# A two-layer hybrid backbone on one core: modulation with its weight stationary, and matmul operands at another place in SBUF

## The chip, the cores and the metric

The kernel runs on one core of a Trainium2 chip. A core has five engines that run side by side: TensorE (PE, with the weight loads shown apart as PEld), VectorE (DVE), ScalarE (ACT), GpSimd (POOL) and SyncE (SP), which here only issues DMA transfers between main memory (HBM) and the on-chip memory SBUF; matmuls write to PSUM. A matmul has a stationary operand, loaded ahead of it, and a moving one that is streamed through. The metric is device time in microseconds; smaller is better. The kernel before takes 3382.59 us (median of three runs).

## The reference

Two groups of tokens, a prompt of 128 and a latent grid of 1024, share the weights of two layers (D = 1024). Of each layer:

```python
def mix_inputs(x, cond, p):
    mod = jax.nn.silu(cond) @ p["w_mod"] + p["b_mod"]
    shift, scale, gate = jnp.split(mod, 3, axis=-1)
    h = rmsnorm(x, p["g_norm"]) * (1 + scale[:, None, :]) + shift[:, None, :]
    parts = jnp.split(h @ p["w_in"], _in_split_points(), axis=-1)
    return gate, parts
...
    # three mixers fed by the parts: bidirectional RG-LRU, latent attention (MLA), windowed attention (SWA)
    u = (m[:, :, 0] * ((y_rnn * jax.nn.silu(g_rnn)) @ p["w_br_rnn"])
         + m[:, :, 1] * ((y_mla * jax.nn.silu(g_mla)) @ p["w_br_mla"])
         + m[:, :, 2] * ((y_swa * jax.nn.silu(g_swa)) @ p["w_br_swa"]))
    out = u @ p["w_out"]
    x = x + gate[:, None, :] * out
```

The modulation `mod` is a vector of 3072 numbers per group and layer: one row of conditions (two, one for each group) times a weight of 1024 x 3072. A final RMSNorm closes the net. All of it is float32 to the accuracy of float32.

## The kernel before

**Large matmuls.** Each operand is split into a high and a low part in the type fp32r, and a product is three matmuls, hi*hi, hi*lo and lo*hi (`mm3`, L232 to L239). Activations lie with features on the partitions; the 1152 tokens (1024 and 128) are cut into three chunks of 384 columns. So the input projection (`in`) is, for each of its blocks of 128 output features and each chunk, 8 x 3 matmuls with 128 stationary weight columns and 384 moving token columns (`hhi`, `hli`; `hhh`, `hlh` for the last chunk). `wo` is the output projection, `mgrnn`, `mgmla` and `mgs` are the merges of the three branches, `tm` the projections that come out with tokens on the partitions.

**Modulation** (`prepare`, L277). The weight of a layer comes in six blocks c of 512 columns, each in four quarters q of 256 rows (two k of 128): `unit(c, q)`. A unit loads its quarter (512 KB) and runs one `piece`: the condition is the stationary operand, four columns wide, and the weight moves, 512 columns, into one row of PSUM per condition, `ps[0:4, :]`. In fp32 the four columns are two conditions and two columns of zeros (`scf`); in fp32r they are the high and the low parts of the conditions (`sc4`) and the weight comes in high and low parts too. When a block is complete, `finish` copies the four rows out (ACT, L319, tile `mr`), turns them by four transposes on PE (L322, tile `modT`) so that features lie on the partitions, and DVE adds the bias (from L324).

Two kinds of units: layer 0's blocks 0 to 3 (16 units, `direct`, plain fp32, L310) run in the opening, since scale and shift must be there before the first activation `hhi` can be made; a float32 matmul that is no transpose shows as two records on PE. The opening also holds the sums of squares of the norm (`ssi`, L395) and the broadcast of the inverse root (`rbi`, L406), both small float32 matmuls between the units. The other 32 units (layer 0's blocks 4 and 5, the gate, and layer 1's six blocks) are the stream G of `filler()` (L763) in layer 0's RNN stage, fp32r, L313 and L314: every third filler runs one piece, between pieces of the input projection and of the gates of the RG-LRU (`g`).

**Order and memory.** In these stages the order of PE (and of DVE, ACT and POOL in some) is written by hand (`manual_schedule`); SP's, and elsewhere the others', comes from a scheduler that knows which buffers share memory: a load into memory that was another tile's is put behind the last use of that tile. Pools are laid one behind the other, so that each tile's size shifts what follows. In the merge of the RNN branch (L861) the eight parts of y are read; the first four stay in SBUF, the last four are reloaded (`yraw`, L904, from `yr` in HBM), cast (`yh`, ACT) and subtracted (`yl`, DVE). Just before it the last 24 blocks of the input projection are put through a sigmoid (`osg`, L734) and stored (`sg`, L735).

## Time and profile before

| | before |
|---|---|
| time, median of 3 runs | 3382.59 us (3379.35 to 3383.43) |
| span of the profiled execution | 3375.3 us |
| PE busy | 3287.6 us (97%) |
| DVE, ACT, POOL busy | 1820.3, 1551.6, 1450.9 us (54, 46, 43%) |
| matmul records on PE | 19572 |
| mean granted TensorE clock | 0.984 |

The profile shows one execution. It gives no time of its own for it besides the span, which runs from the first to the last instruction; the median is 7.3 us longer. Busy times of PE overlap from one matmul to the next, because matmuls are pipelined, so that a listed duration is longer than the distance from one start to the next. In a row of the timeline stand start and duration in us, engine, line, operation, output <- inputs, size (partitions x stationary columns, partitions x moving columns), count, and in brackets the idle time before it with what ended it. A granted clock of 1.00 is 2.4 GHz, one of 0.50 is 1.2 GHz.

### The profile page before, as it was taken

The page shows a single profiled execution, that of the slowest core. Times are in us where ns is not written, and L with a number is a line of the kernel's source. Part 1 is how long each engine was busy: PE and PEld are TensorE (multiplying, and loading weights), DVE is VectorE, ACT ScalarE, POOL GpSimd, SP SyncE. Part 2 cuts the span into 40 slices and gives each one's busy share as a digit, 9 for nine tenths or more (in the row PEclk, how much of TensorE's full clock was granted, in tenths as well). Part 3 has the DMA queues.
Part 4 walks back from the last instruction along what each step waited for, and adds up shares of the span by engine and source line. Part 5 has one row for each costly group of instructions (what it writes and reads, how often), then busy time and mean ns, then how long its engine had stood idle before and what let it go on. Part 6 is the DMA issues. An engine that isn't in the chain of part 4 may idle for free. (4 is left out here: it accounts for less than half of the span.)

```text
span 3375.3 us, 52189 instructions
## 1 busy us (share of the span) xinstructions
PE 3287.6 (97%) x19572; PEld 3095.7 (92%) x19572; DVE 1820.3 (54%) x3254; ACT 1551.6 (46%) x3061; POOL 1450.9 (43%) x1174
## 2 busy tenths in 40 slices
PE   7999999999999999999999999999999999999998
PEld 4999999999998998778989999999999999977898
DVE  6345443332327888667563444423332588876766
ACT  4344444434226777554243433333341477765532
POOL 3655554433214444445374445333331244434543
PEclk9999999999999999899999999999999999989999
DMA  5333232232441002446432222222244200234563
GB/s 209 100 99 97 95 119 92 94 99 94 153 155 30 25 25 68 125 135 229 169 114 91 77 79 81 81 73 82 85 132 135 86 28 27 51 103 119 171 201 134
DMA packets 246652, 351.06 MB, mean 104 GB/s; under 512 B 73216, under 2 KB 200832, under 8 KB 246144
## 3 DMA queue, kind: packets, MB, share of 16 engines
q1 hardware_dynamic: 246400, 347.74, 32.5%
q8 instruction: 154, 2.52, 0.3%
q14 instruction: 98, 0.80, 0.1%
HBM read 248.88 MB, written 98.78 MB: 103 GB/s over the span
## 5 line engine op out<-in xcount | busy, mean ns | idle before, releaser
L239 PE MATMUL in<-hhi,wh_in 128*128 128x384 f32 x1536 | 524.0, 341 | 6.0 <-ACT osg L734 4.4
L239 PE MATMUL in<-hli,wh_in 128*128 128x384 f32 x1536 | 522.6, 340 | 1.6 <-DVE hli L427 1.6
L239 PE MATMUL in<-hhi,wl_in 128*128 128x384 f32 x1536 | 521.9, 340 | 0.0
L215 POOL TENSOR_TENSOR wl_in<-wr_in,wh_in 128x1024 fp32r<-128x1024 f32 x94 | 235.4, 2506 | 329.3 <-ACT wh_in L209 254.1
L239 PEld LDWEIGHTS in<-hhi,wh_in 128*128 128x128 f32 x1536 | 290.0, 189 | 6.8 <-ACT osg L734 5.0
L239 PEld LDWEIGHTS in<-hli,wh_in 128*128 128x128 f32 x1536 | 289.8, 189 | 3.9 <-DVE hli L427 3.9
L239 PEld LDWEIGHTS in<-hhi,wl_in 128*128 128x128 f32 x1536 | 289.9, 189 | 0.0
L239 PE MATMUL in<-hlh,wh_in 128*128 128x384 f32 x768 | 261.6, 341 | 2.8 <-DVE hlh L427 2.8
L239 PE MATMUL in<-hhh,wl_in 128*128 128x384 f32 x768 | 261.3, 340 | 2.0 <-POOL wl_in L215 2.0
L239 PE MATMUL in<-hhh,wh_in 128*128 128x384 f32 x768 | 261.5, 340 | 0.3 <-ACT osg L734 0.3
L1169 POOL TENSOR_SCALAR p<-p,mx 128x1152 f32<-128x1152 f32 x128 | 158.2, 1236 | 200.9 <-DVE mx L1166 126.4
L1220 DVE TENSOR_TENSOR pl<-pt,ph 128x512 fp32r<-128x512 f32 (+1 forms) x320 | 201.4, 636 | 29.8 <-ACT ph L1216 27.1
L1216 ACT CAST ph<-pt 128x512 fp32r<-128x512 f32 (+1 forms) x320 | 170.1, 552 | 92.4 <-PE pt L1209 87.9
L610 DVE SCALAR_TENSOR_TENSOR r<-r,txl 128x1156 f32<-128x1156 f32 x16 | 31.4, 1962 | 320.9 <-ACT r L609 320.9
L1209 PE MATMUL pt<-ident,p 128*128 128x128 f32 x1152 | 169.7, 274 | 9.5 <-DVE kl L1079 4.1
L734 ACT ACTIVATE osg<-in 128x384 f32<-128x384 f32 x144 | 69.0, 489 | 237.3 <-PE in L239 154.9
L1209 PEld LDWEIGHTS pt<-ident,p 128*128 128x128 f32 x1152 | 133.2, 141 | 32.6 <-DVE pl L1220 10.5
L209 ACT CAST wh_in<-wr_in 128x1024 fp32r<-128x1024 f32 x96 | 99.9, 1044 | 126.2 <-PE in L239 91.6
L1234 PE MATMUL o<-ph,v 128*128 128x256 f32 x576 | 153.2, 293 | 0.0
L239 PEld LDWEIGHTS in<-hlh,wh_in 128*128 128x128 f32 x768 | 145.0, 189 | 4.3 <-DVE hlh L427 4.3
L239 PEld LDWEIGHTS in<-hhh,wl_in 128*128 128x128 f32 x768 | 144.9, 189 | 2.3 <-POOL wl_in L215 2.3
L1234 PE MATMUL o<-pl,v 128*128 128x256 f32 x576 | 145.7, 280 | 0.0
(451 smaller groups left out, 9652.5 us busy)
## 6 DMA issues: line engine op xcount, KB each, us to landing
wr_in<-in_w_fm SPq DMA_DIRECT2D x96, 512.0 KB, 3.6
sg<-osg SPq DMA_DIRECT2D x144, 192.0 KB, 1.9
wr_wm<-in_w_mod SPq DMA_DIRECT2D x32, 512.0 KB, 4.0
wr_wo<-in_w_out SPq DMA_DIRECT2D x32, 512.0 KB, 3.7
yr<-gsil SPq DMA_DIRECT2D x16, 576.0 KB, 2.8
msgrnn<-sg SPq DMA_DIRECT2D x48, 192.0 KB, 2.4
u<-msgrnn SPq DMA_DIRECT2D x48, 192.0 KB, 2.5
qr<-qs SPq DMA_DIRECT2D x36, 256.0 KB, 3.9
```

The costliest lines, as they stand in the source:

```text
L209: nc.scalar.copy(out=hi, in_=src)
L215: eng.tensor_tensor(out=lo, in0=src, in1=f(hi), op=ALU.subtract)
L239: nc.tensor.matmul(ps, x, y, start=n == 0, stop=n == last)
L610: nc.vector.scalar_tensor_tensor(out=rr[d], in0=rr[d], scalar=1.0, in1=tt[d], op0=ALU.add, op1=ALU.mult)
L734: nc.scalar.activation(out=o, in_=ps, func=ACT.Sigmoid)
L1169: nc.gpsimd.tensor_scalar(out=pts[i], in0=pts[i], scalar1=mxs[i][:, 5:6], scalar2=1.0, op0=ALU.mult, op1=ALU.mult)
L1209: nc.tensor.transpose(ps[:, w:w + P], pts[q][:, k * P:(k + 1) * P], ident)
L1216: nc.scalar.copy(out=r["h", j][:, 0:width(j)], in_=r["t", j][:, 0:width(j)])
L1220: nc.vector.tensor_tensor(out=r["l", j][:, 0:width(j)], in0=r["t", j][:, 0:width(j)], in1=f(r["h", j][:, 0:width(j)]), op=ALU.subtract)
L1234: nc.tensor.matmul(O[:, 0:256], V[k][:, h % 4, :], x[:, 256 * i:256 * i + 256], start=k == 0 and e == 0, stop=k == 8 and e == 1)
```

## The change

It has two parts.

**Modulation.** The operands change places: 128 columns of the weight become stationary and the four condition columns move. A `piece` runs over two k, four blocks i of 128 columns and, in fp32r, the two parts of the weight. The result comes out with features on the partitions, `ps[:, 4 * i:4 * i + 4]`, so the copy `mr` and the transposes `modT` go; DVE reads the result as before.

On PE in the opening, layer 0's blocks 0 to 3; `wm` is a quarter of the weight, `scf` the conditions. Before:

```order
L310 MATMUL mod_0_196<-wm_0_119,scf 4x512 x2
L310 MATMUL mod_0_196<-wm_1_121,scf 4x512 x2
L310 MATMUL mod_0_196<-wm_2_125,scf 4x512 x2
L310 MATMUL mod_0_196<-wm_3_127,scf 4x512 x2
L395 MATMUL ssi_228<-ones,ssai_201 128x1 x3
L322 MATMUL modT_0_241<-ident,mr_0_239 128x4 x4
L310 MATMUL mod_1_250<-wm_0_129,scf 4x512 x2
L310 MATMUL mod_1_250<-wm_1_131,scf 4x512 x2
L406 MATMUL rbi_255<-dgi_235,ones 128x128 x3
```

Now:

```order
L314 MATMUL mod_0_200<-scf,wm_0_123 128x4 x8
L314 MATMUL mod_0_200<-scf,wm_1_125 128x4 x8
L314 MATMUL mod_0_200<-scf,wm_2_129 128x4 x8
L314 MATMUL mod_0_200<-scf,wm_3_131 128x4 x8
L392 MATMUL ssi_256<-ones,ssai_217 128x1 x3
L314 MATMUL mod_1_271<-scf,wm_0_133 128x4 x8
L314 MATMUL mod_1_271<-scf,wm_1_135 128x4 x8
L403 MATMUL rbi_288<-dgi_263,ones 128x128 x3
```

Each quarter has eight matmuls of four moving columns in place of two of 512; the small matmuls of the norm stand where they stood, and the transposes are gone.

On PE in the stream, one piece of layer 0's block 4. Before:

```order
L313 MATMUL mod_4_1000<-wh_wm_4_0_930,sc_98 4x512
L314 MATMUL mod_4_1000<-wl_wm_4_0_931,sc_98 4x512
L313 MATMUL mod_4_1000<-wh_wm_4_0_930,sc_98 4x512
L314 MATMUL mod_4_1000<-wl_wm_4_0_931,sc_98 4x512
L239 MATMUL g_0_000_1012<-xh_0_899,wh_lru_0_539 128x384
```

Now the piece is sixteen matmuls, of which the first and last are:

```order
L314 MATMUL mod_4_1072<-sc_102,wh_wm_4_0_1002 128x4
L314 MATMUL mod_4_1072<-sc_102,wl_wm_4_0_1003 128x4
L314 MATMUL mod_4_1072<-sc_102,wh_wm_4_0_1002 128x4
L314 MATMUL mod_4_1072<-sc_102,wl_wm_4_0_1003 128x4
...
L314 MATMUL mod_4_1072<-sc_102,wl_wm_4_0_1003 128x4
```

Four matmuls became sixteen, at the same place among the others; there are 32 such pieces.

**Layout.** A small tile of 96 bytes (`edge`) at the right end, widths of 1216 in place of 1156 and 1160 elements (`AW`), another order of pools (`ep` behind `mdp`, with `rows` and `rope` in it) and a pool of its own for `mx` move the operands of the large matmuls. By the addresses that the two builds give them, before, the moving operands of the input projection and of `wo` begin at 224 bytes mod 256 and their weights at 128, others at 192, 64, 0 or 32, and those of the wide merge at 128; now moving and stationary operands of all large fp32r matmuls are at 128, but for 480 of `mgs`, whose weights stay at 224 (tile starts; the columns read begin at multiples of 256 behind them). No loop over data and no size of a transfer changes by it.

One order changes by it, on SP's queue at layer 0's merge: `sg` are the stores of the gates, `yraw` the reloads of y. Before:

```order
L735 DMA sg_19_470<-osg 128x384
L827 DMA yrb_1_7330<-yr_2_440 128x1152
L827 DMA yrb_1_7330<-yr_3_441 128x1152
L629 DMA yr_7_445<-gsil_7_6672 128x1152
L735 DMA sg_19_470<-osg 128x384 x2
L904 DMA yraw_6_7875<-yr_6_444 128x1152
L904 DMA yraw_7_7879<-yr_7_445 128x1152
L904 DMA yraw_4_7883<-yr_4_442 128x1152
L222 DMA wr_rnn_0_7911<-in_w_br_rnn 128x1024
L735 DMA sg_20_471<-osg 128x384 x3
```

Now:

```order
L732 DMA sg_22_545<-osg 128x384 x3
L732 DMA sg_23_546<-osg 128x384 x2
L845 DMA msgrnn_0_0_8398<-sg_0_523 128x384
L845 DMA msgrnn_0_1_8402<-sg_0_523 128x384
L732 DMA sg_23_546<-osg 128x384
L845 DMA msgrnn_0_2_8406<-sg_0_523 128x384
L901 DMA yraw_6_8275<-yr_6_516 128x1152
L901 DMA yraw_7_8279<-yr_7_517 128x1152
L901 DMA yraw_4_8283<-yr_4_514 128x1152
L907 DMA krt_8295<-in_rope_k 128x512
```

The three reloads went from among the stores of sg_19 to behind the last store of sg_23; in the new build their memory overlaps the `osg` buffers. Layer 1 keeps its place for them.

The diff, with repeated changes of width left out:

```diff
@@ -25,6 +25,7 @@
 NCH = 3
 XW = 1160
 RW = 1156
+AW = 1216
 CTX = 1027
 EPS = 1e-6
 BIG = float(2.0 ** 100)
@@ -196,6 +197,7 @@
             kw["side"] = side
         return stack.enter_context(tc.tile_pool(name=name, bufs=bufs, reuse_waits="tile", **kw))
 
+    pool("edge", side="right").tile([P, 24], F32, name="edge")
     base = pool("base")
     wp = pool("wp", bufs=2)
     dr = pool("dr", space=DRAM)
@@ -304,22 +306,17 @@
                 if q == 0:
                     st["ps", c] = psd.tile([P, 512], F32, tag="d", name=f"mod{l}_{c}")
                 ps = st["ps", c]
+                parts, x = ((w,), scf) if direct else (w, sc4)
                 for k in range(2):
                     kk = 2 * q + k
-                    if direct:
-                        nc.tensor.matmul(ps[0:4, :], scf[:, kk, :], w[:, k, :], start=kk == 0, stop=kk == 7)
-                        continue
-                    wh, wl = w
-                    nc.tensor.matmul(ps[0:4, :], sc4[:, kk, :], wh[:, k, :], start=kk == 0, stop=False)
-                    nc.tensor.matmul(ps[0:4, :], sc4[:, kk, :], wl[:, k, :], start=False, stop=kk == 7)
+                    for i in range(4):
+                        for z, part in enumerate(parts):
+                            nc.tensor.matmul(ps[:, 4 * i:4 * i + 4], part[:, k, i * P:(i + 1) * P], x[:, kk, :],
+                                             start=kk == 0 and i == 0 and z == 0, stop=kk == 7 and z == len(parts) - 1,
+                                             skip_group_check=True)
 
             def finish():
                 ps = st["ps", c]
-                mr = base.tile([4, 512], F32, tag="mr", name=f"mr{l}_{c}", bufs=1)
-                nc.scalar.copy(out=mr, in_=ps[0:4, :])
-                ps = psd.tile([P, 512], F32, tag="d", name=f"modT{l}_{c}")
-                for i in range(4):
-                    nc.tensor.transpose(ps[:, 4 * i:4 * i + 4], mr[:, i * P:(i + 1) * P], ident[0:4, 0:4])
                 mo = base.tile([P, 4, 4], F32, tag="mo", name=f"mo{l}_{c}", bufs=2)
                 nc.vector.tensor_copy(out=mo, in_=ps[:, 0:16].rearrange("p (a b) -> p a b", b=4))
                 nc.vector.tensor_tensor(
@@ -536,15 +533,15 @@
         with ExitStack() as rst:
             rp = pool(f"rnn{l}", stack=rpst)
             fp = pool(f"fw{l}", bufs=2, stack=rst)
-            ep = pool(f"ev{l}", bufs=2, stack=rst)
             tp = pool(f"tm{l}", stack=rst)
             mdp = pool(f"md{l}", bufs=1, stack=rst)
+            ep = pool(f"ev{l}", bufs=2, stack=rst)
             psr = pool(f"psr{l}", bufs=3, space=PSUM, stack=rst)
-            rows = tp.tile([P, R_N], F32, name=f"rows{l}")
+            rows = ep.tile([P, R_N], F32, name=f"rows{l}", bufs=1)
             nc.sync.dma_start(out=rows, in_=a["rows"][l])
-            rope = tp.tile([P, 8, 2, 64], F32, name=f"rope{l}")
+            rope = ep.tile([P, 8, 2, 64], F32, name=f"rope{l}", bufs=1)
             nc.sync.dma_start(out=rope, in_=a["rope_s"])
-            xpads = [rp.tile([P, XW], F32, tag="xpad", name=f"xpad{l}")]
+            xpads = [rp.tile([P, AW], F32, tag="xpad", name=f"xpad{l}")[:, 0:XW]]
             for x in xpads:
                 nc.gpsimd.memset(x[:, 0:1], 0.0)
                 nc.gpsimd.memset(x[:, 1 + NL:CTX + 1], 0.0)
@@ -561,15 +558,15 @@
                         return
                     nc.scalar.copy(out=xp[:, 1 + c * CH:1 + NL], in_=ps[:, 0:NL - c * CH])
                     nc.scalar.copy(out=xp[:, CTX + 1:CTX + 1 + P], in_=ps[:, NL - c * CH:CH])
-                    xc = rp.tile([P, RW], F32, tag="xc", name=f"xc{l}_{ft}")
+                    xc = rp.tile([P, AW], F32, tag="xc", name=f"xc{l}_{ft}")[:, 0:RW]
                     nc.vector.tensor_scalar(out=xc, in0=xp[:, 0:RW], scalar1=cw[:, 0:1],
                                             scalar2=sv[:, V_CB + ft:V_CB + ft + 1], op0=ALU.mult, op1=ALU.add)
                     for k in range(1, 4):
                         nc.vector.scalar_tensor_tensor(out=xc, in0=xp[:, k:k + RW], scalar=cw[:, k:k + 1], in1=xc,
                                                        op0=ALU.mult, op1=ALU.add)
                     r["xc"] = xc
-                    r["xh"] = rp.tile([P, RW], F32R, tag="xh", name=f"xh{l}_{ft}")
-                    r["xl"] = rp.tile([P, RW], F32R, tag="xl", name=f"xl{l}_{ft}")
+                    r["xh"] = rp.tile([P, AW], F32R, tag="xh", name=f"xh{l}_{ft}")[:, 0:RW]
+                    r["xl"] = rp.tile([P, AW], F32R, tag="xl", name=f"xl{l}_{ft}")[:, 0:RW]
                     split(r["xh"], r["xl"], xc, "act", "pool")
 
                 def ev_g(c, ps):
...
@@ -822,7 +819,7 @@
                     raw = xp2.tile([P, KT, 384], F32, tag="twl", name=f"yrb{l}_{g}").rearrange("p k n -> p (k n)")
                     for j in range(2):
                         k, y = 2 * g + j, raw[:, j * T:(j + 1) * T]
-                        ys[k] = [rp.tile([P, T], F32R, tag=t, name=f"y{t}{l}_{k}")
+                        ys[k] = [rp.tile([P, T if t == "gsil" else AW], F32R, tag=t, name=f"y{t}{l}_{k}")[:, 0:T]
                                  for t in (("r0", "r1"), ("i0", "i1"), ("xc", "xh"), ("xl", "gsil"))[k]]
                         nc.sync.dma_start(out=y, in_=yr_d[k])
                         split(*ys[k], y, "act", "dve")
@@ -1028,6 +1025,7 @@
             SA, SB = (pss.tile([P, 1024], F32, name=f"s{x}{l}") for x in "ab")
             SM = pss.tile([P, 512], F32, name=f"sm{l}")
             mq = pool(f"mlaq{l}", bufs=2, stack=mqst)
+            mqs = pool(f"mlas{l}", bufs=2, stack=mqst)
             tab = pool(f"tab{l}", stack=mqst).tile([P, 2, T], F32, name=f"tab{l}")
             nc.sync.dma_start(out=tab, in_=a["qtab"])
             st = {}
@@ -1142,7 +1140,7 @@
 
                 def rmax(i, e, S):
                     if e == 0:
-                        mxs[i] = mq.tile([P, 8], F32, tag=f"mx{i}", name=f"mx{l}_{h}_{pr}_{i}", bufs=3)
+                        mxs[i] = mqs.tile([P, 8], F32, tag=f"mx{i}", name=f"mx{l}_{h}_{pr}_{i}", bufs=3)
                     nc.vector.tensor_reduce(out=mxs[i][:, e:e + 1], in_=S, axis=AX.X, op=ALU.max, negate=True)
 
                 def low(i):
@@ -1620,7 +1618,7 @@
                     M.do(t, u)
                 cst.close()
                 box["sqa"] = pool(f"swaa{l}", bufs=2, side="right", stack=ast)
-                box["snk"] = box["sqa"].tile([P, 8], F32, name=f"snk{l}", bufs=1)
+                box["snk"] = box["sqa"].tile([P, 64], F32, name=f"snk{l}", bufs=1)[:, 0:8]
                 nc.sync.dma_start(out=box["snk"], in_=a["rows"][l][:, R_SINK:R_SINK + 8])
                 for t in range(3):
                     k_load(t)
```

## Rows read from the trace of the kernel before

**Rows 1.** The page's busy times: engine, busy us, share of the span, instructions.

```profile
PE 3287.6 (97%) x19572; PEld 3095.7 (92%) x19572; DVE 1820.3 (54%) x3254; ACT 1551.6 (46%) x3061; POOL 1450.9 (43%) x1174
```

**Rows 2.** Stretches: length, busy us (count) of PE, PEld, DVE, ACT, POOL; clock; DMA.

```profile
9.86:44.80 34.94, 31.24 (x97) 8.49 (x95) 21.25 (x62) 11.99 (x23) 5.06 (x4) 1.00 0.91 346
124.00:908.00 784.00, 782.76 (x4668) 763.16 (x4667) 293.06 (x354) 322.98 (x485) 359.57 (x229) 1.00 0.32 103
1344.40:1351.30 6.90, 6.90 (x36) 4.93 (x34) 5.30 (x14) 4.19 (x12) 4.93 (x6) 1.00 0.54 131
1351.30:1375.20 23.90, 23.90 (x74) 17.48 (x73) 12.99 (x30) 11.07 (x26) 7.52 (x9) 0.50 0.44 145
3365.50:3368.30 2.80, 1.62 (x6) 1.36 (x6) 0.75 (x4) 0.00 (x0) 0.60 (x1) 0.50 0.00 0
```

**Rows 3.** Timeline, all engines, the end of the opening.

```profile
44.87 0.57 ACT L319 COPY mr<-mod 4x512 f32<-4x512 f32 x1 [4.61 <-PE mod L310]
45.94 0.17 DVE L324 COPY mo<-modT 128x16 f32<-128x16 f32 x1 [0.29 <-PE modT L322]
47.52 0.69 PE L239 MATMUL in<-hhi,wh_in 128*128 128x384 f32 x1 [1.62 <-ACT hhi L424]
```

**Rows 4.** Timeline, weight loads and matmuls with few columns.

```profile
18.38 0.74 PEld L395 LDWEIGHTS ssi<-ones,ssai 128*128 128x128 f32 x6 [1.59 <-DVE ssai L387]
47.52 0.29 PEld L239 LDWEIGHTS in<-hhi,wh_in 128*128 128x128 f32 x1 [1.71 <-ACT hhi L424]
1137.07 0.19 PEld L239 LDWEIGHTS sx<-kl,qh 128*128 128x128 f32 x1
1137.29 0.19 PEld L239 LDWEIGHTS sa<-kh,qh 128*128 128x128 f32 x1
3366.54 1.36 PEld L406 LDWEIGHTS rbend<-dgend,ones 128*128 128x128 f32 x6 [1.65 <-issue]
```

**Rows 5.** Timeline, PE, first matmul of a streamed unit and first behind it.

```profile
814.77 0.39 PE L313 MATMUL mod<-wh_wm,sc 128*4 128x512 f32 x1
815.70 0.34 PE L239 MATMUL g<-xh,wh_lru 128*128 128x384 f32 x1
```

**Rows 6.** Timeline, PE, around a streamed block's transposes; their durations, ns min/median/max.

```profile
829.66 0.34 PE L239 MATMUL in<-hli,wh_in 128*128 128x384 f32 x1
830.10 0.41 PE L322 MATMUL modT<-ident,mr 4*128 4x4 f32 x4
831.07 0.34 PE L239 MATMUL in<-hhi,wh_in 128*128 128x384 f32 x1
L322 PE MATMUL modT<-ident,mr x48: 197/198/221, 19.1 to 830.3; 4*128 4x4 f32 x48
```

**Rows 7.** Timeline, PE, dense stretches of input projection and wide merge, ends only.

```profile
889.81 0.34 PE L239 MATMUL in<-hhi,wh_in 128*128 128x384 f32 x1
894.40 0.34 PE L239 MATMUL in<-hhi,wl_in 128*128 128x384 f32 x1
915.71 0.33 PE L861 MATMUL mgrnn<-yh,wh_rnn 128*128 128x384 f32 x1
920.74 0.34 PE L861 MATMUL mgrnn<-yh,wl_rnn 128*128 128x384 f32 x1
```

**Rows 8.** Layer 0's merge: timeline, landing of yraw, the page's row for sg.

```profile
866.24 0.88 SPq L904 DMA_DIRECT2D yraw<-yr  x2
909.12 0.32 SPq L735 DMA_DIRECT2D sg<-osg  x1
910.17 5.16 DVE L215 TENSOR_TENSOR yl<-yraw,yh 128x1152 fp32r<-128x1152 f32 x4 [44.01 <-ACT yh L209]
914.66 0.34 PE L861 MATMUL mgrnn<-yh,wh_rnn 128*128 128x384 f32 x1
DMA to landing us min/median/max: 3.5/4.7/6.7
sg<-osg SPq DMA_DIRECT2D x144, 192.0 KB, 1.9
```

More of the change, by code (lines that the diff above doesn't have):

```diff
@@ L586, in gate @@
                         t = "ri"[g] + str(d)
-                        r[t] = rp.tile([P, RW], F32, tag=t, name=f"{t}{l}_{ft}")
+                        r[t] = rp.tile([P, AW], F32, tag=t, name=f"{t}{l}_{ft}")[:, 0:RW]
                     dst, vb = r["ri"[g] + str(d)], (V_BA, V_BI)[g]
@@ L601, in scan @@
                     rr, ii = [r["r0"], r["r1"]], [r["i0"], r["i1"]]
-                    tt = [f(rp.tile([P, RW], F32R, tag=t, name=f"t{t}{l}_{ft}")) for t in ("xh", "xl")]
+                    tt = [f(rp.tile([P, AW], F32R, tag=t, name=f"t{t}{l}_{ft}")[:, 0:RW]) for t in ("xh", "xl")]
                     gsil = r["gsil"]
@@ L783, in late_norm @@
             def late_norm():
-                va = rp.tile([P, RW], F32, tag="i1", name="va")
-                vb = rp.tile([P, RW], F32, tag="xc", name="vb")
+                va = rp.tile([P, AW], F32, tag="i1", name="va")[:, 0:RW]
+                vb = rp.tile([P, AW], F32, tag="xc", name="vb")[:, 0:RW]
                 acc = va[:, 0:CH]
@@ L902, in _backbone @@
                         else:
-                            raw = rp.tile([P, XW], F32, tag="xpad", name=f"yraw{l}_{k}")[:, 0:T]
+                            raw = rp.tile([P, AW], F32, tag="xpad", name=f"yraw{l}_{k}")[:, 0:T]
                         nc.sync.dma_start(out=raw, in_=yr_d[k])
```

## The prediction

> **What bounds the kernel now.** I read the page's first part first: PE is busy for 97% of the span, 3287.6 us [rows 1], so the question at every stretch is how long PE's own instructions are. Then the table of stretches: through the input projection of layer 0 (124 to 908 us) PE is busy for 782.76 of 784.00 us, at a granted clock of 1.00, while DVE, ACT and POOL are each under half busy [rows 2]. What is put on PE there lengthens the kernel by its whole length, and what is taken off shortens it. The opening, where layer 0's first four blocks of modulation are computed, is PE's as well: 31.24 of 34.94 us [rows 2]. Its end is a chain: the last modulation matmul, a copy on ACT, a transpose, a copy on DVE, the scaling, and at 47.52 us the first matmul of the input projection [rows 3]. The third view is the timeline of PE, for the distance from one matmul's start to the next, which is what a matmul costs in a dense stretch (its listed duration overlaps the next one).
>
> The page gives no time of its own for the profiled execution, only the span, 3375.3 us; the median of the three runs is 3382.59, so 7.3 us lie around the span. I sum against the span and add 7.3.
>
> **Part 1, the opening.** Before: 32 fp32 matmuls, two records each, with 512 columns moving. After: 128 of them, 256 records, each of which loads 128 stationary columns and then streams four. What one costs is then a weight load. The nearest row is the reduction of the squares (ssi, one column moving, 128 stationary, fp32): six loads fill 0.74 us, that is five distances and a last load of about 0.19, so 0.11 us each [rows 4]. At a granted clock of 0.50 the same kind of matmul (rbend near the end of the kernel) has six loads in 1.36 us; a load at that clock lasts 0.29 [rows 4], so (1.36 - 0.29) / 5 = 0.214 us each. The stretch at 3365.50 shows that clock [rows 2].
>
> So everything hangs on which clock the opening gets. The rows that tell are those around 1351 us. From 1344.40 to 1351.30 PE is busy for 6.90 of 6.90 us, 36 records of matmuls, and yet in the stretch that follows the clock is 0.50 (1.2 GHz), again with PE never idle (23.90 of 23.90) [rows 2]. Being occupied did not keep the clock. Those matmuls are scores and transposes of the attention with 128 columns or more, one in 0.19 us (6.90 / 36); four columns in 0.11 us are far less, so I take 0.50 for the whole opening. Then PE needs 256 x 0.214 = 54.8 us for the modulation and 24 x 0.214 = 5.1 for the four groups of ssi and rbi between its units (24 records by the order). PE starts at 6.8 as before (the first weights' landing), and the later weights now land ahead of it, so it ends at 6.8 + 54.8 + 5.1 = 66.7 instead of just before 44.87. Behind the last matmul the ACT copy and the transposes are gone: the copy on DVE came 45.94 - 44.87 = 1.07 us after the ACT copy's start [rows 3] and now follows PE directly, about 0.95 earlier. First projection matmul: 47.5 + 21.9 - 0.95 = 68.5. **+21.0 us**, with nothing to hide it, since all of layer 0 waits for the scaling. The other bound is the full clock: 280 x 0.11 = 30.8, an end at 37.6 and -8 in all, if the loads and the squares on DVE, on which ssi and rbi wait in PE's order, came earlier too; if these keep their times, only the 0.95 us and a little more are won, -1.4.
>
> **Part 2, the 32 streamed units.** Before: four matmuls of 512 columns per unit, 815.70 - 814.77 = 0.93 us [rows 5], 32 x 0.93 = 29.8. After: 16 matmuls of four columns. In fp32r the nearest are three sx matmuls in a row with 128 stationary and 128 moving columns, whose loads start 1137.07 and, two later, 1137.29 [rows 4]: 0.11 us each. 512 x 0.11 = 56.3 us. PE has no slack there [rows 2], so **+26.4 us**. Lower bound: the four-row transposes, four in 0.41 us of which the last takes 0.20, so 0.07 each [rows 6], which gives +6. They load four rows where these load 128, so I stay with sx. Upper bound: the clock. A unit lasts 1.8 us among some 15 us of 384-column matmuls; a fall in each would cost up to 18 us more. I give that little weight.
>
> **Part 3, transposes.** The eight finishes inside the stream go. Around the last, five input matmuls and the transposes take 831.07 - 829.66 = 1.41 us [rows 6]; five such matmuls alone take 5 x 0.1765 = 0.88. 8 x 0.53 = **-4.2 us**. Their ACT copies lay beside PE and were worth nothing. Those of the opening are in part 1.
>
> **Part 4, the layout.** Before, the moving operands of the input projection and of wo lie at 224 mod 256 and their weights at 128; the wide merge has both at 128. In the input projection 26 distances take 894.40 - 889.81 = 4.59 us, 176.5 ns each; in the merge 29 take 920.74 - 915.71 = 5.03 us, 173.4 ns [rows 7]. Same shape, same type, same clock. If the places are the cause, each of 6912 input and 1152 wo matmuls gains 3.1 ns: 21.4 + 3.6 = 25.0. Some 5,700 others (tm, q, scores, g, the narrow merges) change place too; between 0 and 3.1 ns each is 0 to 18, and I take half, 9, since many of them stream only 256 columns. **-34 us**; bounds 0 (the places are not the cause) and -43. PE is the bound wherever these lie.
>
> The Trainium skill speaks against this part: "SBUF — State Buffer", section Specifications, gives SBUF lines of 16 bytes, with a penalty for crossing to a new line. 224 and 128 both begin such a line, so by that page the move would gain nothing, and the sum would come out 34 us higher; the rows above show a difference of 3 ns between just these two places.
>
> **Part 5, a transfer that moves.** With the new addresses the buffers of yraw_6, yraw_7 and yraw_4 in layer 0 lie over those of the last gate outputs (osg), and their loads on SP's queue go from the middle of the gates (866.24) to behind the last gate's store. That store is issued at 909.12 and such a store lands in 1.9 us (median), so the first load is issued at 911.0; landing takes 4.7 (3.5 to 6.7); the subtraction on DVE takes 1.3 (four in 5.16), and the cast on ACT before it is taken to last as long [rows 8]. The high part is ready at 917.0 and the low part at 918.3, where PE wanted the first at 914.66 [rows 8]: **+4 us**, rounded up to 4.4 for what the idle clock may cost; 0 to +7. Queued behind those loads on SP are small loads of the attention (krt, rck), which nobody needs yet. Layer 1 keeps its order. The order of the other engines changes only by neighbours, at nothing: they are under half busy there.
>
> **Sum.** +21.0 + 26.4 - 4.2 - 34 + 4.4 = +13.6 on the span: 3388.9, and with 7.3 around it **3396 us**.
>
> **Rivals.**
> (a) *The opening keeps its clock.* Then part 1 is -1.4 instead of +21.0: 3396 - 22.4 = 3374, on the faster side. With the other bound it is 3367. This decides alone: with the other parts as summed, before and after tie where the opening ends 13.6 us earlier than I say, at (66.7 - 13.6 - 6.8) / 280 = 0.165 us a record, and below that the kernel is faster. For it: PE will be occupied without a pause, and 1.00 was granted there before. Against: the fall at 1351 with PE never idle [rows 2].
> (b) *The places are not the cause*, or only half of it. Then part 4 is between 0 and -17: 3430 or 3413. For it: the two stretches differ also in their tiles and in what else runs beside them [rows 7].
> (c) *A narrow matmul costs less than a full weight load*, about the 0.07 us of a four-row transpose [rows 6]. Then part 2 is +6, and part 1 at the lower clock ends at 256 x 0.14 + 24 x 0.214 + 6.8 = 47.8, which makes it +2. 3396 - 20 - 19 = 3357. Against: the loads in both types [rows 4]. The Trainium skill's page "TensorE: Matmul & The Clock Gate", section Back-to-back issue gap, has a table by which 1 to 64 columns cost about 60 cycles, an estimated 25 ns; by it parts 1 and 2 together would be a gain. The ssi rows, with one column at 0.11 us, go against its use here.
> (d) *The stream loses the clock at each unit*: up to +18, 3414. Against: transposes of 0.5 us inside the same stream left the clock at 1.00 [rows 2].
> (e) *The moved loads cost nothing*, because the landing is quicker: 3392. It changes no verdict.
>
> **How the numbers follow.** My forecast with (e): 0.70; (a) 0.08; (b) 0.10; (c) 0.05; (d) 0.07. A measurement of this kernel can tell about 0.2%, 6.8 us, so "same" is 3375.8 to 3389.4. Faster: (c), most of (a), and a tail where the other 5,700 matmuls gain in full and the stall is absent: 0.15. Same: the lower side of the forecast, where the layout gives -43 and the units cost a little less than a full load: 0.20. Slower: 0.65. The range, 3371 to 3414, reaches to (a) below and to half of (b) and to (d) above; (c) and the whole of (b) are left out.
>
> **What would show it.** In the profile after: the granted clock between 10 and 68 us, 0.50 or 1.00, and the start of the first input matmul (68.5 by me, 46 by rival a); the distance of the four-column matmuls, 0.11 us in the stream and 0.214 in the opening; the distance in the input projection, 173.4 or still 176.5 ns; an idle stretch of PE in the wide merge, released by yh or yl, of about 4 us; 1.00 as granted clock throughout the stream. The forecast is wrong if the opening ends before 60 us or if the input projection still runs at over 175 ns.

## The result: slower by 0.8%, and where it shows in the profile

The changed kernel takes 3407.86 us (median of four runs, 3406.71 to 3412.93) where the kernel before takes 3381.73 beside it: 26.1 us or 0.8% slower, ratio 1.0083 with an interval of 1.0068 to 1.0097. The profiled execution has a span of 3405.8 us against 3375.3, 30.5 longer. After the change a run of 3407.61 us has the span 3405.8, so that 1.8 us lie around a span; by that the profiled execution of before took about 3377 us (an estimate, 3375.3 + 1.8), less than any of the four runs beside it (3379.35 to 3383.43). I compare the two profiles with each other and keep in mind that the medians stand 4 us closer.

PE is as full as before (the page: engine, busy us, share of the span, instructions), with 20100 matmul records in place of 19572 [rows 1]:

```profile
PE 3316.9 (97%) x20100; PEld 3169.9 (93%) x20100; DVE 1828.5 (54%) x3254; ACT 1550.6 (46%) x3051; POOL 1451.2 (43%) x1174
```

**The opening.** Timeline of the changed kernel: start and duration in us, engine, line, output <- inputs, count, and in brackets the idle time and its releaser.

```profile
39.30 1.42 PE L314 MATMUL mod<-scf,wm 128*128 128x4 f32 x6
67.85 0.17 DVE L321 COPY mo<-mod 128x16 f32<-128x16 f32 x1 [8.22 <-PE mod L314]
69.43 0.69 PE L241 MATMUL in<-hhi,wh_in 128*128 128x384 f32 x1 [1.62 <-ACT hhi L421]
```

Six four-column matmuls fill 1.42 us, which is five distances and a last one of 0.35: 0.213 us each. DVE copies the result straight from PSUM, and the first input matmul starts at 69.43, 21.9 us later than before [rows 3]. The clock column is no witness here: it shows 1.00 for these stretches only because this trace has no entry of the clock before 74.4 us. The distance, 0.213 us, is the one that the rows of before show at 0.50 [rows 4].

**The stream.** One unit, from its first matmul to the first behind it:

```profile
849.22 0.17 PE L314 MATMUL mod<-sc,wh_wm 128*128 128x4 f32 x1
850.92 0.42 PE L241 MATMUL g<-xh,wh_lru 128*128 128x384 f32 x1
```

1.70 us where it was 0.93 [rows 5]. With the first matmuls behind it, which start later too, the same matmul behind a unit stands 0.84 to 0.87 us later than before against the one ahead of it, at 31 of the 32 units (0.55 at the first).

**The input projection**, 125 distances in a dense stretch, its ends:

```profile
923.36 0.33 PE L241 MATMUL in<-hhi,wl_in 128*128 128x384 f32 x1
945.02 0.33 PE L241 MATMUL in<-hli,wh_in 128*128 128x384 f32 x1
```

21.66 us for 125 distances is 173.3 ns, where it was 176.5 [rows 7]. The same two matmuls before, 22.09 us apart, 176.7 ns a distance:

```profile
885.39 0.34 PE L239 MATMUL in<-hhi,wl_in 128*128 128x384 f32 x1
907.48 0.34 PE L239 MATMUL in<-hli,wh_in 128*128 128x384 f32 x1
```

The page's groups say the same of the listed durations (busy us, mean ns of one, idle before):

```profile
L241 PE MATMUL in<-hhi,wh_in 128*128 128x384 f32 x1536 | 516.9, 337 | 8.6 <-ACT osg L731 7.0
L1232 PE MATMUL o<-ph,v 128*128 128x256 f32 x576 | 154.9, 294 | 0.0
```

337 ns against 341 in the kernel before. But the second row, the product of the MLA's probabilities with v, went the other way, from 293 to 294 ns.

**Layer 0's gates**, a wait that the kernel before has too, but shorter. The first row is the kernel before, the others the changed kernel:

```profile
865.86 0.44 PE L239 MATMUL in<-hhi,wh_in 128*128 128x384 f32 x1 [1.24 <-ACT osg L734]
890.98 0.44 PE L241 MATMUL in<-hhi,wh_in 128*128 128x384 f32 x1 [0.78 <-ACT osg L731]
893.45 0.80 SPq L824 DMA_DIRECT2D yrb<-yr  x2
900.03 1.15 ACT L211 CAST yxl<-yrb 128x1152 fp32r<-128x1152 f32 x1 [1.25 <-DMA yrb<-yr]
902.04 0.86 ACT L731 ACTIVATE osg<-in 128x384 f32<-128x384 f32 x2
902.57 0.44 PE L241 MATMUL in<-hhi,wh_in 128*128 128x384 f32 x1 [2.97 <-ACT osg L731]
```

PE waits 2.97 us for the sigmoid `osg`, because ACT works in order and stands at the cast `yxl`, which waits for the second of the `yrb` loads. Ahead of 890.98 PE lay 34.1 us behind its place of before, and 38.2 us behind it after this wait: 0.78 us of idle time at 890.98 that the kernel before doesn't have, 1.7 us more here, and an entry of the clock at 0.50 from 903.8 to 907.2.

**Layer 0's wide merge**, the moved loads:

```profile
949.01 1.27 SPq L901 DMA_DIRECT2D yraw<-yr  x3
952.96 1.15 ACT L211 CAST yh<-yraw 128x1152 fp32r<-128x1152 f32 x1 [5.28 <-DMA yraw<-yr]
954.16 0.44 PE L858 MATMUL mgrnn<-yh,wh_rnn 128*128 128x384 f32 x1 [1.87 <-ACT yh L211]
955.55 0.69 PE L858 MATMUL mgrnn<-yl,wh_rnn 128*128 128x384 f32 x1 [0.95 <-DVE yl L217]
955.00:958.40 3.40, 2.85 (x9) 2.85 (x10) 3.03 (x3) 1.91 (x2) 0.00 (x0) 0.50 0.38 109
```

Issued at 949.01, cast at 952.96: PE idles 1.87 us for the high and 0.95 for the low part, and then runs at 0.50 for the 3.4 us of the last row (its columns are those of [rows 2]). In [rows 8] PE met the same matmul at 914.66 with no idle time. This costs 4.6 us, of which 1.3 come back some 15 us later at a transpose (`trck`), for which PE idled 1.12 us before and no longer waits.

### The profile page after: what moved, and what is told of

Its sections match the earlier page's. It is cut to its first block, busy times and chain, and to the rows that moved or that the text cites. A ratio compares the mean times of both kernels' runs of the same rounds, so it can differ in the third digit from the quotient of the medians.

```text
span 3405.8 us, 53234 instructions
## 1 busy us (share of the span) xinstructions
PE 3316.9 (97%) x20100; PEld 3169.9 (93%) x20100; DVE 1828.5 (54%) x3254; ACT 1550.6 (46%) x3051; POOL 1451.2 (43%) x1174
## 5 line engine op out<-in xcount | busy, mean ns | idle before, releaser
L241 PE MATMUL in<-hhi,wh_in 128*128 128x384 f32 x1536 | 516.9, 337 | 8.6 <-ACT osg L731 7.0
L1167 POOL TENSOR_SCALAR p<-p,mx 128x1152 f32<-128x1152 f32 x128 | 157.7, 1232 | 200.4 <-DVE mx L1164 126.0
```

The source lines that it names most:

```text
L241: nc.tensor.matmul(ps, x, y, start=n == 0, stop=n == last)
L1167: nc.gpsimd.tensor_scalar(out=pts[i], in0=pts[i], scalar1=mxs[i][:, 5:6], scalar2=1.0, op0=ALU.mult, op1=ALU.mult)
```

## The experiments

Each stands against runs of the kernel before on the same chip. In what follows, "old form" is the modulation as before (512 columns moving, transposes), "new form" that of the change. SBUF has no room for both the new layout and the tile `mr`; where the old form is used in another layout, `mr` is a slot of the weight ring:

```diff
-                mr = base.tile([4, 512], F32, tag="mr", name=f"mr{l}_{c}", bufs=1)
+                mr = wview(wp.tile([P, 8, P], F32, tag="wr", name=f"mr{l}_{c}", bufs=3), 1, 512)[0:4, 0, :]
```

### One half of the change at a time

**The layout without the new modulation.** The changed kernel with `piece` and `finish` of the kernel before:

```diff
-                parts, x = ((w,), scf) if direct else (w, sc4)
...
+                    if direct:
+                        nc.tensor.matmul(ps[0:4, :], scf[:, kk, :], w[:, k, :], start=kk == 0, stop=kk == 7)
+                        continue
...
+                    nc.tensor.transpose(ps[:, 4 * i:4 * i + 4], mr[:, i * P:(i + 1) * P], ident[0:4, 0:4])
```

> The new layout with the old modulation (512 columns moving, transposes; the four copied rows lie in a slot of the weight ring). My theory, that the parts add up as the two traces show them: the input projection at 173.4 ns a matmul instead of 176.5 (-22 us), wo -4, nothing from the other matmuls, and the moved yraw loads +4: about 3360 us, 3355 to 3366. Rival, that the shorter distances come from something else than the layout: 3382 or, with the stall, 3386 us.

3367.15 us, ratio 0.9952 (0.9935 to 0.9968): faster than before by 0.5%, less than expected (3360), with runs from 3360.7 to 3375.2. The stall at `yh` is there as in the changed kernel:

```profile
912.83 0.63 PE L863 MATMUL mgrnn<-yh,wh_rnn 128*128 128x384 f32 x1 [1.96 <-ACT yh L211]
914.22 0.69 PE L863 MATMUL mgrnn<-yl,wh_rnn 128*128 128x384 f32 x1 [0.77 <-DVE yl L217]
```

The profile is that of the slowest of the four runs (3375.24 us); it has 134.7 us in entries of 0.50, where that of before has 107.8. So the layout is the part that gains, and the loss of the whole change lies in the modulation.

**The new modulation without the layout.** `piece` and `finish` of the change in the kernel before:

```diff
+                parts, x = ((w,), scf) if direct else (w, sc4)
...
+                            nc.tensor.matmul(ps[:, 4 * i:4 * i + 4], part[:, k, i * P:(i + 1) * P], x[:, kk, :],
...
-                    nc.tensor.transpose(ps[:, 4 * i:4 * i + 4], mr[:, i * P:(i + 1) * P], ident[0:4, 0:4])
```

> The new modulation with the old layout. My theory: the opening at half clock +22, the 32 streamed units +27, eight transposes with their copies -5.6: about 3425 us, 3420 to 3430; first input matmul at 69.4 us; distance in the input projection still 176.5 ns; no idle PE at yh. Rival, that part of the loss belongs to the layout (the stall at the gates around 902 us and the clock after it): 3418 us or less.

3427.89 us, ratio 1.0139 (1.0124 to 1.0155), 47 us slower, as expected (3425). Its first input matmul stands at 69.01, and the wait at the gates is there without the layout:

```profile
913.28 0.44 PE L239 MATMUL in<-hhi,wh_in 128*128 128x384 f32 x1 [2.79 <-ACT osg L729]
```

2.79 us idle. So that wait grows without the new places in SBUF, too. The input projection runs at 176.6 ns a distance here, as in the kernel before. The moved loads belong to the layout: here they stand where they stood, and PE does not wait at `yh`.

**The opening alone in the old form.** In the changed kernel, for the 16 units of the opening only:

```diff
+                if direct:
...
+                            nc.tensor.matmul(ps[0:4, :], scf[:, kk, :], w[:, k, :], start=kk == 0, stop=kk == 7)
...
+                    return
                 parts, x = ((w,), scf) if direct else (w, sc4)
```

> The changed kernel, only the 16 units of the opening in the old form (512 columns moving, transposes). My theory: all of the opening's loss comes back, 3408 - 22 = 3386 us, first input matmul at 47.5 us, granted clock 1.00 from about 10 us on. Rival, that DVE and POOL, which run ahead during the longer opening, then hold up the start of the input projection: 3390 to 3396 us.

3390.16 us (median of seven, 3380.76 to 3394.35; ratio 1.0026, 1.0014 to 1.0038), 17.7 us under the changed kernel's median and not the 22 that were expected. The opening itself came back whole, with the first input matmul at 47.42. But the wait at the gates is longer here:

```profile
884.01 0.69 PE L241 MATMUL in<-hhi,wh_in 128*128 128x384 f32 x1 [3.79 <-ACT osg L747]
```

3.79 us, the longest of all kernels; the profile holds 127.8 us at 0.50 (after the change 111.3). Why the wait is longer than in the changed kernel is left open. The rival (that DVE and POOL hold up the start of the projection) isn't what happened: in time the value is the rival's, in place it is not.

**The stream alone in the old form.** The same switch for the other 32 units:

```diff
+                if not direct:
...
+                        nc.tensor.matmul(ps[0:4, :], sc4[:, kk, :], wh[:, k, :], start=kk == 0, stop=False)
+                        nc.tensor.matmul(ps[0:4, :], sc4[:, kk, :], wl[:, k, :], start=False, stop=kk == 7)
+                    return
```

> The changed kernel, only the 32 streamed units in the old form (512 columns moving, transposes; the four copied rows in a slot of the weight ring). My theory: the stream's 27 us less the 5.6 of the transposes come back, and with them the stall at the gates around 902 us (3.4): 3408 - 25 = 3383 us, 3380 to 3387. Rival, that the stall at the gates belongs to the layout: 3386 to 3389 with an idle PE of 3 us ahead of the gates' matmul as in the changed kernel.

3387.83 us (ratio 1.0015, 1.0005 to 1.0025), 20 us under the changed kernel, not 25. First input matmul at 68.96, so the opening costs its 21.4 us alone as well. At the gates 2.03 us of idle time are left, between the 1.24 of before and the 2.97 after:

```profile
883.04 0.44 PE L241 MATMUL in<-hhi,wh_in 128*128 128x384 f32 x1 [2.03 <-ACT osg L747]
```

A part of that wait thus is the layout's and a part the modulation's, and neither theory has it right. The kernels with the old modulation and a faster projection show the layout's part: the wait is 1.91 us in layout_only and 2.05 to 2.18 in layout_ep, edge96, edge32, edge64 and left96 (the last five below). Of edge96:

```profile
860.55 0.50 PE L240 MATMUL in<-hhi,wh_in 128*128 128x384 f32 x1 [2.09 <-ACT osg L735]
```

### Which clock the opening gets

**Two blocks in the old form, then two in the new.**

```diff
+                if direct and c < 2:
...
+                            nc.tensor.matmul(ps[0:4, :], scf[:, kk, :], w[:, k, :], start=kk == 0, stop=kk == 7)
...
+                    return
```

> The changed kernel with the first two of the opening's four blocks in the old form, the last two in the new, stream as changed. Theory clock: the old form gets 1.00 granted by about 10 us as before; the four-column matmuls that begin near 29 us run at 0.112 us until the clock is taken back to 0.50 some us later, then at 0.213 to the end; the profile shows an entry of 0.50 between 29 and 56 us, and the first input matmul stands at 50 to 58 us. Rival, that an fp32 load of 128 columns into PE takes 0.21 us in this place whatever the clock (other traffic, the place of the weights): 0.213 us from the first one on, at a granted clock of 1.00. Third possibility, that PE's occupation keeps the clock: 0.112 us to the end and first input matmul at 46 to 48 us.

3397.09 us, a single run. The timeline (first the last of the old matmuls, then new ones, the small transposes of block 1, and new ones again) and the stretches, columns as in [rows 2]:

```profile
24.64 2.74 PE L313 MATMUL mod<-wm,scf 128*4 128x512 f32 x6
28.34 0.92 PE L324 MATMUL mod<-scf,wm 128*128 128x4 f32 x7
29.53 1.79 PE L324 MATMUL mod<-scf,wm 128*128 128x4 f32 x8
12.60:29.60 17.00, 15.50 (x63) 5.90 (x61) 7.95 (x19) 9.16 (x19) 0.86 (x1) 1.00 1.04 402
29.70:55.70 26.00, 26.00 (x123) 26.00 (x124) 15.06 (x53) 2.37 (x3) 3.93 (x3) 0.50 0.67 248
```

The old form runs at full clock, 0.43 us a record (six in 2.74, the last 0.59). The first sixteen of the new form, from 27.31 on, have distances of 0.111 and 0.112 us (the first 0.133). At 29.6 the trace has the entry of 0.50, and from there to the end of the opening each of the new matmuls takes 0.213 or 0.214, although PE is busy for 26.00 of 26.00 us. First input matmul at 57.69. That is the theory of the clock, step for step. The rival, that such a load costs 0.21 us in this place whatever the clock, falls with the first sixteen, and the third possibility with all the others.

**The new form with wide matmuls between.** In the changed kernel, an unused matmul of the old form (496 columns, into a part of the same PSUM tile that nobody reads) ahead of every eight new ones; for the second kernel the condition is `if direct`, one ahead of every four:

```diff
+                    if direct and k == 0:
+                        nc.tensor.matmul(ps[0:4, 16:512], scf[:, kk, :], w[:, k, 16:512], start=kk == 0, stop=False,
+                                         skip_group_check=True)
```

> The changed kernel with one matmul of the old form (496 columns moving, two records, its result not used) ahead of every eight new ones in the opening: 16 of them. Theory clock (the opening is slow because few columns are streamed and the clock stays at 0.50): if one in eight is enough, the clock is granted 1.00 within the opening, the four-column matmuls fall from 0.213 to 0.112 us, and the opening gets shorter although it does more, first input matmul at 53 us; if it is not enough, 0.213 us throughout and first input matmul at 95 us. Rival, that an fp32 weight load of 128 columns takes 0.21 us here whatever the clock: 0.21 us also where the clock is granted 1.00.

> As warm_opening with twice as many: one unused matmul of the old form ahead of every four new ones, 32 in all, which is all the streaming that the old opening had. Theory clock: 1.00 granted, 0.112 us a four-column matmul, first input matmul near 66 us, before the changed kernel's 69.4 although every matmul of it is still there. Rival: 0.21 us whatever the clock, first input matmul at 90 us or later.

3430.69 and 3460.45 us, single runs. In neither did the clock rise: the four-column matmuls stay at 0.213 us, and first input matmuls stand at 97.36 and 126.77. The wide matmuls themselves show the clock, whose first entry in the trace of the second kernel comes at 134.0; of that kernel:

```profile
58.48 1.81 PE L313 MATMUL mod<-wm,scf 128*4 128x496 f32 x2
60.23 1.87 PE L317 MATMUL mod<-scf,wm 128*128 128x4 f32 x8
```

Two records of 496 columns from 58.48 to 60.23 are 0.87 us each, twice the 0.43 that they take in the old opening. So the opening stayed at the lower clock with all the wide matmuls of the old opening put between the narrow ones. The expectation that the second kernel would rise was wrong, and what the clock of the opening hangs on stays open; these two don't tell the clock from the load by themselves, which opening_half does.

### The places in SBUF

**Only the right end moved.** The kernel before with one tile (and `mr` in the weight ring, as above), nothing else of the layout:

```diff
+    pool("edge", side="right").tile([P, 24], F32, name="edge")
     base = pool("base")
```

> The kernel before with one tile of 96 bytes at the right end of SBUF (and the four copied rows of the modulation in a slot of the weight ring, for room): the moving operands of the input projection and of wo go from 224 to 128 mod 256, their weights stay at 128, nothing else of the layout is widened or reordered. Theory place (128 is a good place for the moving operand): input projection 173.5 ns a matmul instead of 176.6, wo likewise, -24 us; the tm matmuls, whose moving weights stay at 224 while their stationary side is now at 128, unchanged or, by the next theory, 3 ns slower (+4 us): 3357 to 3362. Rival, that the gain of the full change needs the rest of the layout: 3375 to 3381.

3360.24 us, ratio 0.9935 (0.9917 to 0.9953): the whole of the layout's gain from one line, 19.0 us under the kernel before, where layout_only is 13.7 under it (their intervals overlap). With layout_ep (below) it is the fastest kernel of this study that was timed in several runs. That `mr` moved is not the cause: mod_only has no `mr` in its old place either and runs the projection at 176.6 ns. The yraw loads stand where they stood.

**Other distances**, 32 and 64 bytes at the right end, and 96 at the left end:

```diff
+    pool("edge", side="right").tile([P, 8], F32, name="edge")
...
+    pool("edge", side="right").tile([P, 16], F32, name="edge")
...
+    pool("edge").tile([P, 24], F32, name="edge")
```

> As edge96 with a tile of 32 bytes: moving operands of the input projection at 192 mod 256, weights at 128. Theory place (only 128 is good): 176.6 ns. Theory step of 64 (a moving operand at a multiple of 64 is as good as at 128, one 32 bytes beside it is slower while the weights lie on such a multiple): 173.5 ns.

> As edge96 with a tile of 64 bytes: moving operands of the input projection at 160 mod 256, weights at 128. Theory place: 176.6 ns. Theory step of 64: 176.6 ns. If every place but 224 is good: 173.5 ns.

> The kernel before with a tile of 96 bytes at the left end: the weights of the input projection go from 128 to 224 mod 256, the moving operands stay at 224. Theory relation (what counts is that both sides lie alike): 173.5 ns. Theory place: 176.6 ns or more, since now both lie at 224.

3361.70, 3368.54 and 3357.02 us (single runs). The same 125 distances of the input projection as above, first and last start; in order edge96, edge32, edge64, left96:

```profile
881.95 0.33 PE L240 MATMUL in<-hhi,wl_in 128*128 128x384 f32 x1
903.61 0.33 PE L240 MATMUL in<-hli,wh_in 128*128 128x384 f32 x1
```

```profile
880.83 0.34 PE L240 MATMUL in<-hhi,wl_in 128*128 128x384 f32 x1
902.50 0.34 PE L240 MATMUL in<-hli,wh_in 128*128 128x384 f32 x1
```

```profile
885.18 0.33 PE L240 MATMUL in<-hhi,wl_in 128*128 128x384 f32 x1
906.85 0.34 PE L240 MATMUL in<-hli,wh_in 128*128 128x384 f32 x1
```

```profile
880.62 0.33 PE L240 MATMUL in<-hhi,wl_in 128*128 128x384 f32 x1
902.28 0.33 PE L240 MATMUL in<-hli,wh_in 128*128 128x384 f32 x1
```

All four are 21.66 or 21.67 us, 173.3 ns a distance, where the kernel before takes 22.09 for the same 125, 176.7. Over all distances between input matmuls at full clock (those over 1.3 times the median left out) the means are (moving place, weights' place, mod 256):

| kernel | moving | weights | layer 0, ns | layer 1, ns |
|---|---|---|---|---|
| before | 224 | 128 | 176.6 | 176.7 |
| edge96 | 128 | 128 | 173.5 | 173.5 |
| edge32 | 192 | 128 | 173.4 | 173.4 |
| edge64 | 160 | 128 | 174.8 | 173.9 |
| left96 | 224 | 224 | 173.5 | 173.5 |

128 is not a special place: 192 is as good, and 224 is good where the weights lie there too. Of the three theories, "place" falls with edge32 and left96; "step of 64" fits edge32 but not edge64, which is near the good ones; "relation" fits left96 but not edge32, where the sides differ. What is shown is that one pair, 224 with 128, is slow, and that four others are not, or little. edge64 is in between only as a mean: its stretches of 100 us lie between 173.3 and 176.0 ns.

The same means for other groups of matmuls say more. edge96 moves the right end by 96 bytes and left96 the left end, so that in both the two sides have moved by 96 bytes against each other, while the places themselves are other ones:

| matmuls, columns | before, ns | edge96, ns | left96, ns |
|---|---|---|---|
| input projection, 384 | 176.6 | 173.5 | 173.5 |
| `wo`, 384 | 176.6 | 173.9 | 173.9 |
| `tm`, 384 | 174.2 | 175.9 | 175.9 |
| `tm`, 256 | 119.8 | 118.5 | 118.5 |
| products with v, 256 | 116.7 | 116.0 | 115.9 |
| merge of MLA, 384 | 173.3 | 174.8 | 174.8 |
| merge of SWA, 384 | 174.8 | 174.0 | 173.9 |

The two kernels agree within 0.1 ns in every group, also where the shift costs time. So it is how the two sides lie to each other that counts here, and not the place of either. The theory "relation" was too narrow in wanting them alike: a difference of 96 bytes is slow in the input projection, 0 and 64 are not, and 32 is slow in some stretches. `tm` with 384 columns, which by the expectation of edge96 gets the pair 224 and 128 there, became 1.7 ns slower; with 256 columns it became faster. Why a difference costs time is left open.

**The new layout without the moved loads.** layout_only with the pool of the gate outputs ahead of the weights of tm, as before the change, and 160 bytes of padding in it:

```diff
             fp = pool(f"fw{l}", bufs=2, stack=rst)
+            ep = pool(f"ev{l}", bufs=2, stack=rst)
             tp = pool(f"tm{l}", stack=rst)
             mdp = pool(f"md{l}", bufs=1, stack=rst)
-            ep = pool(f"ev{l}", bufs=2, stack=rst)
...
+            ep.tile([P, 40], F32, name=f"pad{l}", bufs=1)
```

> As layout_only (new layout, old modulation), but with the pool of the gate outputs (osg) in front of the weights of tm, 160 bytes of padding in it, so that all operands stay at 128 mod 256 and the yraw buffers no longer overlap osg; the yraw loads stand among the stores of sg_19 again. My theory: no idle PE at yh in layer 0, 4 us less than layout_only, about 3356 us. Rival, that the loads are late for another reason: the same time as layout_only.

3361.55 us, ratio 0.9945 (0.9923 to 0.9966), 5.6 under layout_only by the medians, whose intervals overlap. In the profile it is plain:

```profile
910.85 0.33 PE L864 MATMUL mgrnn<-yh,wh_rnn 128*128 128x384 f32 x1
```

no idle time ahead of the first matmul with `yh`; the loads go out at 861.27, where layout_only issues them at 907.58. The stall in the changed kernel comes from the overlap of memory, as the order on SP's queue said.

## The prediction, step by step

The forecast was 3396 us, slower, with a range of 3371 to 3414; 3407.86 came. The direction is right and the reasons for it are the ones given, but the change costs about 26 us and not 14. Of the 7.3 us that the forecast adds around the span only 1.8 lie there; the rest is that the profiled execution of before was a short one. By parts, from where the same matmuls stand in the two profiles:

| part | forecast, us | found, us |
|---|---|---|
| 1 opening | +21.0 | +21.9 |
| 2 stream, 32 units | +26.4 | +27.1 |
| 3 transposes, 8 finishes | -4.2 | -4.3 |
| 4 layout | -34 | -24.8 |
| 5 moved loads | +4.4 | +3.4 |
| gates of layer 0 | 0 | +4.2 |
| other waits and the clock elsewhere | 0 | +3.0 |

The last row is what is left of the 30.5 us by which the two profiles differ; the medians are 26.1 apart. Measured alone, the layout is worth -13.7 us (layout_only against before) and the new modulation +47.1 (mod_only), together 33.4, 7 more than the whole change. The modulation agrees with its rows (21.9 + 27.1 - 4.3 = 44.7, and a longer wait at the gates). The layout does not: its rows with the moved loads give -21.4. layout_only's four runs spread over 14.5 us, and the difference stays open.

**1, right.** Half clock, 0.213 us a record, the end within 1 us of the forecast; opening_half shows the same load at 0.112 and at 0.213 us, one after the other, and the entry of the clock between them. Rival (a) is out. That few columns were the reason for the lower clock is not shown: warm_opening_2 streamed the old opening's columns among the narrow matmuls and stayed at 0.213 us.

**2, right.** 0.112 us a matmul was measured where 0.11 was taken; the difference to 26.4 is the first matmuls behind each unit. Rival (c), a cheap narrow matmul, is out: no matmul here with a full weight load of its own came below 0.11 us in a row; only the second of a unit follows its first by 0.03 us. With that goes the use of the figure that the Trainium skill's page "TensorE: Matmul & The Clock Gate" (Back-to-back issue gap) gives for 1 to 64 columns. Rival (d) is out as well: between 142.6 and 903.8 us the trace has no entry of 0.50. The 18 us that I gave it come from no row.

**3, right**: 0.54 us a finish, with the first matmuls behind it, where the rows around one gave 0.53.

**4, the step that failed: the size of the rest.** Here I take the distance from each matmul to the next in both profiles, where both run at a granted clock of 1.00 and PE does not idle. The input projection gained 3.1 ns at 6762 such distances, 21.1 us (forecast 21.4), `wo` 2.6 ns at 1144, 3.0 us (3.6). For the 5,700 other matmuls I took half of 3.1 ns each, 9 us. All other groups together gained 0.7 us: the products with v lost 1.8 ns at 1172 distances (2.2 us) and the MLA merge 0.8 us, and no group won more than 0.7 (the SWA merge 0.7, `tm` 0.5). The working took over for them what rows 7 show of one pair of places, though their pairs were other ones; left96, edge32 and edge64 show that this pair was the slow one of five, and the table of edge96 and left96 that the same shift costs other groups time. For the same reason rival (b) is half right: 128 is not the cause, that the two sides no longer lie as 224 and 128 to each other is. The rule of the Trainium skill's page "SBUF — State Buffer" (Specifications) is one of lines of 16 bytes, and all these places begin such a line. It doesn't explain the 3 ns, and neither do the experiments.

**5, right** in mechanism and place: issue at 949.01, 2.4 us behind the last gate's store at 946.65 (1.9 forecast), the cast 3.95 us later, 2.8 us of idle time and a piece of lower clock behind it. layout_ep takes the overlap away and the stall goes.

**Not forecast: the gates.** The wait at `osg` grew from 1.24 to 2.97 us, and one of 0.78 us ahead of it is new. PE's order is fixed, but ACT's cast `yxl` waits for a load that goes out when DVE has read the buffer before it. That load went out at 893.45, 36.2 us later than before, while PE itself lay 35.0 us behind; the cast came another 0.6 us later. mod_only (2.79), stream_old (2.03) and the kernels with a faster projection alone (1.91 to 2.18) share it out to both halves of the change. I had written that the other engines, under half busy, hide this; the place where they don't was in the trace of before, with its own idle time. That DVE's chain is later because its last gates stand behind streamed units is only argued.

**Behind it.** Behind the wide merge of layer 0 the two profiles run level to the end of the SWA merge, 40.5 to 42.6 us apart, and `wo` wins 1.4 us back. In layer 1 the projection wins 10 us back, the attention and merges lose some 5 and `wo` wins 2 to 3; of the loss the entries of 0.50 (111.3 us against 107.8 in all) are a part. The lower clock falls on other places there in each of the kernels, so I don't give that loss to the change.

## What to carry to other kernels

A matmul with few moving columns cost its weight load here, 0.112 us among wide matmuls at full clock and 0.213 us in an opening made of little else, at half the clock: count with the second before making a weight stationary to save a transpose. Where a dense stretch runs at 176 ns and another of the same shape at 173, move one operand by 32 or 96 bytes and look again; one such line gave 0.65% here (edge96), while the reordering that came with the full layout gave part of it back through a buffer that now overlapped another. A gain that was measured at one pair of places is not to be counted for groups whose operands lie otherwise: the same shift made `tm` with 384 columns slower.

## What the runs showed of the hardware that was not expected

- The place of the moving operand against the weights in SBUF is worth 3 ns of 176 in fp32r, at one pair (224 and 128 mod 256) of the five that were tried. Moving the one side or the other by 96 bytes gave the same distances within 0.1 ns in seven groups of matmuls (edge96, left96).
- TensorE stayed at half its clock for 120 us in warm_opening_2, by the distances of its matmuls (0.213 and 0.87 us), with PE busy for 118.35 of 119.20 us (6.8 to 126.0) and wide matmuls among the narrow ones; the first entry of 1.00 stands at 134.0.
- The clock column of a stretch reads 1.00 where the trace has no entry yet; distances between matmuls are the safer witness there.
